# Key copies of attention and indexer: the second partition half written by a DMA instead of by casts and subtractions

## The chip, the cores and the metric

One core of a Trainium2 chip runs the whole kernel. The metric is device time in microseconds from start to end of one execution; where a single number is given for a kernel it is the median of the runs shown. The engines are named PE (TensorE), DVE (VectorE), ACT (ScalarE), POOL (GpSimd) and SP (SyncE).

## The reference

One transformer layer, everything in float32, with 512 tokens and 2048 channels:

```python
h = rms_norm(x, norm_attn[l]) * (1.0 + sc1) + sh1
qa, ka, va, qb, ckv, qi, ki, wi = jnp.split(h @ w_in[l], SPLIT_POINTS, axis=-1)
...
out_a = swa_attention(qa, ka, va, attn_sinks[l], rel_a)
out_b = dsa_attention(qb, ckv, w_uk[l], w_uv[l], qi, ki, wi, rel_b)
mix = jnp.concatenate([out_a, out_b], axis=-1) @ w_out[l]
x = x + g1 * mix
h = rms_norm(x, norm_ffn[l]) * (1.0 + sc2) + sh2
x = x + g2 * conv_ffn(h, w_up[l], conv_w[l], conv_b[l], w_down[l])
```

The six vectors sh1, sc1, g1, sh2, sc2, g2 are silu(c) times a 2048 × 12288 matrix, the modulation weights. Group A has 16 query heads of 64 channels on 2 key heads, with a sliding window of 128. Group B has 16 heads of 64 channels whose keys come from a latent of 256 channels through a matrix of each head, and each query attends to 256 keys at most. Which ones they are is decided by the indexer: 16 small query heads against one key head of 64 channels, a weighted sum of relu(dots), and a top-k of the sums.

## The kernel before, in words

Each float32 operand of a product is split into a high half, rounded to the type that PE multiplies at full rate, and a low half, the rest. A product is three matmuls: high × high, high × low, low × high.

For the scores there is a shorter form. A head has 64 channels, and PE contracts over 128 partitions. `stack_q` therefore puts the high half of a head's queries in one set of 64 partitions and the low half in the other. The keys stand in all 128 partitions, twice the same 64 rows, once for the high half (`kh`) and once for the low half (`kl`). `score` needs two matmuls then: stacked queries × `kh` and stacked queries × `kl`. So each key head is wanted in both partition halves. `dup_k` makes it: two casts on ACT (lines 626 and 627) write the high half into the two partition halves, and two subtractions on DVE (lines 629 and 630) write the low half. It is called 19 times: once for the indexer's keys `ki`, out of PSUM; twice for the A-heads' keys `ka`, out of SBUF; and twice, once a head, for each pair of B-heads `kb0` to `kb7`, out of PSUM.

The stages by time in the trace: to 190 us the first projections; to 290 us the indexer's dot products (`dots`) and first A-heads; to 384 us the top-k on DVE (lines 685 and 688, tiles `top` and `wk`) beside the other A-heads (scores `sca`, weights `sa`, transposed weights `tpa` and `eta`) and the first B-head projection; to 570 us eight pairs of B-heads; then the output projection, the up projection to 1700 us and the down projection to the end.

A pair i of B-heads runs like this. The projection makes its queries (`qb`). `prep_gen` makes the keys in PSUM (`kbp`) and calls `dup_k` for each head. The scores (`scb`) follow, then the softmax on DVE and ACT (`sb`); the weights are transposed by PE into PSUM (`tpb`), copied by ACT to SBUF (`etb`, line 826), and multiplied with the values (`o`). While one pair is in its softmax, PE computes the projection of the next. The two heads of a pair come one after the other.

The order of the work on each engine is made by a scheduler at build time, from priorities and from estimated durations; at run time each engine runs its list in order, and waits. A stream of modulation weights runs beside all of this: POOL issues transfers of 512 KB (`mraw`, line 1520) into a ring of three buffers, and DVE sums them up (`macc`, line 231). POOL issues the next one when DVE has freed a buffer.

The tile of the B-heads' keys has one buffer. Keys of the next pair are written when the scores of the last one are done.

Of the kernel before, what the change touches and what calls it, by code (L numbers as in the profile page):

```python
# [8 lines left out]
F32 = mybir.dt.float32  # L9
F32R = mybir.dt.float32r  # L10
AF = mybir.ActivationFunctionType
OP = mybir.AluOpType
# [21 lines left out]
def hybrid_trunk(ctx, tc, xT, cT, wm, bm, nrm, wik, wiq, wi1, sinks, kvn, wuk, wuv, rel, onehot,  # L34
                 wo, wup, cw, cb, wdn, out):
    nc = tc.nc
    act, dve, pe, pool, sp = nc.scalar, nc.vector, nc.tensor, nc.gpsimd, nc.sync
# [46 lines left out]
    def bank(tag, name, shape=(P, T)):  # L84
        if tag == "sc":
            sc_turn[0] += 1
            tag = f"sc{sc_turn[0] % 3}"
        return psp.tile(list(shape), F32, tag=tag, bufs=banks.get(tag, 1), name=name)
# [63 lines left out]
    def toeplitz(g, head, n):  # L152

        return bass.AP(tensor=biasd.tensor, offset=biasd.offset + 2048 * (HEADS * g + head) + 384 * g + P - 1,
                       ap=[[1024 - 64, 2], [-1, 64], [1, n]])

    ki_ps = bank("acc", "ki_ps")
# [10 lines left out]
    def split(raw, lo, n, name):  # L168
        hi_t = ring.tile([P, 512], F32R, tag="whi", bufs=4, name=f"{name}h")
        lo_t = ring.tile([P, 512], F32R, tag="wlo", bufs=4, name=f"{name}l")  # L170
        act.copy(hi_t[:, :n], raw[:, lo:lo + n])
        dve.tensor_tensor(lo_t[:, :n], raw[:, lo:lo + n], hi_t[:, :n].bitcast(F32), OP.subtract)
        return hi_t, lo_t

    def mm3(ps, wh, wl, ah, al, start, stop):
        pe.matmul(ps, wh, ah, start=start, stop=False)
        pe.matmul(ps, wh, al, start=False, stop=False)
        pe.matmul(ps, wl, ah, start=False, stop=stop)
# [7 lines left out]
    def rstd_of(*a, **k):  # L186
        return list(rstd_parts(*a, **k))[1]
# [26 lines left out]
    def split_to(hi_t, lo_t, full, keep=False):  # L214
        hi = act.copy(hi_t, full)  # L215
        if keep:
            tc.keep_in_program_order(hi)
        dve.tensor_tensor(lo_t, full, hi_t.bitcast(F32), OP.subtract)  # L218
# [77 lines left out]
    def start(gen, delay=0, low=False):  # L296
        def run():
            for _ in range(delay):
                yield
            yield from gen  # L300
        (idle if low else active).append(run())
# [301 lines left out]
    def tp_ps(name, shape=(P, 4, P)):  # L603
        return bank("tp", name, shape)

    def tmp_t(name, shape=(P, T)):
        return p1.tile(list(shape), F32, tag="tmp", bufs=2, name=name)

    def stack_q(ps, scale, name):
        q = p1.tile([P, 2, T], F32R, tag="q", bufs=2, name=name)  # L610
        for h in range(2):
            own, other = slice(64 * h, 64 * h + 64), slice(64 - 64 * h, 128 - 64 * h)
            act.mul(q[own, h], ps[own], scale)
            dve.scalar_tensor_tensor(q[other, h], ps[own], scale, q[own, h].bitcast(F32),
                                     OP.mult, OP.subtract)
        return q
# [5 lines left out]
            pe.matmul(ps, identr, hide, start=False, stop=False)  # L622
        pe.matmul(ps, q[:, h, qc], kl[:, k0:k1], start=False, stop=True)

    def dup_k(src, row, kh, kl):
        act.copy(kh[0:64], src)
        act.copy(kh[64:128], src)
        o = kh[row:row + 64]
        dve.tensor_tensor(kl[0:64], src, o.bitcast(F32), OP.subtract)
        dve.tensor_tensor(kl[64:128], src, o.bitcast(F32), OP.subtract)  # L630

    ETS = 4

# [1 line left out]
    ki = p1.tile([P, 4, T], F32R, tag="k", bufs=1, name="ki")  # L635
# [83 lines left out]
    va = p1.tile([P, NB, P], F32, name="va")  # L719
    ka = p1.tile([P, 4, T], F32R, tag="ka", bufs=1, name="ka")  # L720
    wit = tmp_t("wit", (16, T))
    dup_k(ki_ps[0:64], 0, ki[:, 0], ki[:, 1])
    act.mul(wit, ki_ps[64:80], 1.0 / 32.0)

    def keys_gen():
        cf, csq = [], []
        for i in range(2):
            cf.append(p1.tile([P, T], F32, tag="s", bufs=2, name=f"cf{i}", padded_shape=[P, 1280]))
            csq.append(p1.tile([P, T], F32, tag="et", bufs=ETS, name=f"csq{i}"))
            act.activation(csq[i], key_ps[f"ckv{i}"], AF.Square)  # L730
            act.copy(cf[i], key_ps[f"ckv{i}"])
        kar = p1.tile([P, T], F32, tag="et", bufs=ETS, name="kar")
        act.copy(kar, key_ps["ka"])
        vat = p1.tile([P, T], F32, tag="et", bufs=ETS, name="vat")
        act.copy(vat, key_ps["va"])
        yield
        krs = p1.tile([P, T], F32, tag="et", bufs=ETS, name="krs")
        act.copy(krs, rstd_of(csq, 256, "kvss", lambda n: tp_ps(n, (P, T)), krs))
        for g in range(2):
            dup_k(kar[64 * g:64 * g + 64], 64 * g, ka[:, 2 * g], ka[:, 2 * g + 1])  # L740
        yield
        tps = tp_ps("vatp")
        for b in range(NB):
            pe.transpose(tps[:, b], vat[:, P * b:P * b + P], ident)
        dve.tensor_copy(va, tps)
        for i in range(2):
            dve.scalar_tensor_tensor(cf[i], cf[i], kvn_sb[:, i:i + 1], krs, OP.mult, OP.mult)
            split_to(ch[:, i], cl[:, i], cf[i])
        yield
# [122 lines left out]
    def out_box(i):  # L872
        box = {}

        def get():
            if "t" not in box:
                box["t"] = bank("o", f"o{i}")
            return box["t"]

        def finish():  # L880
            if i < 8:
                mixa[i] = ix.tile([P, T], F32, tag=f"m{i}", name=f"mixa{i}")
                act.copy(mixa[i], get())
                return
            if "mh" in env:
                split_to(env["mh"][:, i], env["ml"][:, i], get())
                env["kept"].add(i)
                return
            mx = tmp_t(f"mx{i}")
            act.copy(mx, get())  # L890
            act.dma_start(mixd[i], mx)
        return get, finish
# [13 lines left out]
    kb, vb = {}, {}  # L906

    def prep_gen(i):
        wr = p1.tile([P, 2 * P], F32, tag="wuk", bufs=1, name=f"wukr{i}")
        sp.dma_start(wr, wuk[i].rearrange("p a b -> p (a b)"))  # L910
        if i % 2 == 0:
            wv = tmp_t(f"wuvr{i}")
            sp.dma_start(wv, wuv[i // 2].rearrange("p a b -> p (a b)"))
        yield
        wh, wl = split(wr, 0, 2 * P, f"wuk{i}")
        yield
        kp = tp_ps(f"kbp{i}", (P, T))
        for r in range(2):
            c = slice(P * r, P * r + P)
            mm3(kp, wh[:, c], wl[:, c], ch[:, r], cl[:, r], r == 0, r == 1)  # L920
        k = p1.tile([P, 4, T], F32R, tag="k", bufs=1, name=f"kb{i}")
        for h in range(2):
            own = slice(64 * h, 64 * h + 64)
            dup_k(kp[own], 64 * h, k[:, h], k[:, 2 + h])
        kb[i] = k
        yield
        if i % 2:
            return
        wh, wl = [t.rearrange("p (a b) -> p a b", a=2) for t in split(wv, 0, 512, f"wuv{i}")]
        yield  # L930
        v = p1.tile([P, NB, 2 * P], F32, tag="v", bufs=2, name=f"vb{i}")
        for half in range(2):
            vp = tp_ps(f"vbp{i}_{half}", (P, 2, 2 * P))
            for b in range(2):
                kc = slice(P * (2 * half + b), P * (2 * half + b) + P)
                for r in range(2):
                    pe.matmul(vp[:, b], ch[:, r, kc], wh[:, r], start=r == 0, stop=False)
                    pe.matmul(vp[:, b], ch[:, r, kc], wl[:, r], start=False, stop=False)
                    pe.matmul(vp[:, b], cl[:, r, kc], wh[:, r], start=False, stop=r == 1)
            act.copy(v[:, 2 * half:2 * half + 2], vp)  # L940
            yield
        vb[i], vb[i + 1] = v[:, :, :P], v[:, :, P:]

    def b_after(i):
        def f(ps):
            q = stack_q(ps, -0.125, f"qb{i}")
            get, finish = out_box(8 + i)
            spans = [(0, 0, 128), (128, 0, 256), (384, 0, 384), (768, 0, 512)]
            heads = [Head(f"b{2 * i + h}", toeplitz(1, 2 * i + h, 512), q, h, kb[i][:, h], kb[i][:, 2 + h], spans,
                          3e38, None, keep, lambda kt, h=h: vb[i][:, kt, 64 * h:64 * h + 64]) for h in range(2)]  # L950
            start(pair_gen(heads, get, finish))
            if i < 7:
                start(prep_gen(i + 1), 1)
        return f
# [572 lines left out]

    start(ahead(index_gen(), 0))
    start(ahead(keys_gen(), 0))
    drive(slots, 0, marks["qb0"] - 4, True)  # L1530
    start(prep_gen(0))
    drive(slots, marks["qb0"] - 4, marks["qb0"], True)
    while idle:
# [212 lines left out]
```

## Time and profile before

| what | value |
|---|---|
| median of 3 runs | 2137.85 us (2136.5 to 2139.96) |
| the profiled execution | 2141.57 us, span 2139.8 us |
| granted clock of TensorE, mean | 0.992 |
| PE busy | 2085.0 us, 97% |
| DVE busy | 1714.8 us, 80% |
| ACT busy | 1139.9 us, 53% |
| POOL busy | 180.8 us, 8% |

A row of the timeline has the start in us, the duration in us, engine, line, operation and tiles, and in brackets the idle time of the engine ahead of it with what ended it. A row of groups has busy time and the mean of one, or, in the view of one tile, the shortest, median and longest duration in ns and the first and last start. A row of stages has the busy time of each engine in a stretch, the granted clock, the share of DMA engines that were busy, and GB/s. Matmuls overlap in the pipeline, so that the duration of one is longer than its distance to the next.

### The profile page before, as it was taken

How to read it: one execution, taken by the hardware profiler on the slowest of the kernel's cores; microseconds unless marked ns; L12 is line 12 of the kernel's file. 1: busy time of each engine (PE TensorE's matmuls, PEld its weight loads, DVE VectorE, ACT ScalarE, POOL GpSimd, SP SyncE). 2: the span in 40 equal slices, each digit the busy share in tenths (PEclk: the TensorE clock that was granted, in tenths of full speed). 3: DMA queues.
4: the chain of work that ended last, by engine and by line, in shares of the span. 5: the costliest groups of instructions: out<-in, count | busy, mean ns of one | idle time of the engine just before them, and what ended most of it. 6: DMA issues, size and time to landing. Idle time of an engine off the chain costs nothing.

```text
span 2139.8 us, 34491 instructions
## 1 busy us (share of the span) xinstructions
PE 2085.0 (97%) x13336; PEld 1834.3 (86%) x13336; DVE 1714.8 (80%) x2522; ACT 1139.9 (53%) x1907; POOL 180.8 (8%) x310
## 2 busy tenths in 40 slices
PE   7999999999999999999999999999999999999987
PEld 4777877777788879999999999999999787777877
DVE  3887899878878788888788888888887897787857
ACT  5324886777722274444444444444444576566544
POOL 0000000111133200000000000000000011111110
PEclk9999999999999999999999999999999999999999
DMA  9773222666699724444444434435434788899883
GB/s 391 272 288 106 55 72 60 193 212 208 197 372 321 235 78 142 155 138 129 148 123 149 148 116 151 149 114 157 139 114 147 272 246 212 225 218 225 207 216 99
DMA packets 125029, 385.18 MB, mean 180 GB/s; under 512 B 14783, under 2 KB 24015, under 8 KB 118080
## 3 DMA queue, kind: packets, MB, share of 16 engines
q1 hardware_dynamic: 84096, 257.16, 36.5%
q0 software_dynamic: 31264, 108.51, 19.4%
q10 hardware_dynamic: 9504, 17.31, 2.1%
q8 instruction: 104, 1.70, 0.3%
q14 instruction: 61, 0.50, 0.1%
HBM read 324.46 MB, written 58.46 MB: 179 GB/s over the span
## 4 chain that ended last, share of the span: by engine, by line
PE 75%; DVE 8%; DMA 7%; issue 5%; ACT 4%; POOL 0%; SPq 0%; DVEq 0%; POOLq 0%; ACTq 0%
PE ux L53 22%; PE uy L53 11%; PE p L53 11%; PE uz L53 6%; PE qip L53 4%; DMA qd<-in_wdn_dram 3%; DMA mraw<-in_wm_dram 2%; DVE wd L218 2%; DMA rawbd<-in_wdn_dram 1%; PE ckv L53 1%; PE mrow L53 1%; DVE wk L688 1%; PE o L53 1%; PE mps L53 1%; DVE top L685 1%
## 5 line engine op out<-in xcount | busy, mean ns | idle before, releaser
L53 PE MATMUL p<-wd,af 128*128 128x512 f32 x1680 | 387.8, 392 | 11.6 <-DVE wd L218 10.6
L53 PEld LDWEIGHTS p<-wd,af 128*128 128x128 f32 x1680 | 314.9, 188 | 84.2 <-DVE wd L218 16.8
L53 PE MATMUL ux<-t_up,wu 128*128 128x256 f32 x2952 | 375.2, 283 | 0.0
L53 PEld LDWEIGHTS ux<-t_up,wu 128*128 128x128 f32 x2952 | 362.9, 192 | 0.9 <-DVE gt L1157 0.2
L53 PE MATMUL uy<-h2h,wu 128*128 128x256 f32 x1312 | 249.6, 283 | 0.0
L53 PEld LDWEIGHTS uy<-h2h,wu 128*128 128x128 f32 x1312 | 210.6, 192 | 0.0
L231 DVE SCALAR_TENSOR_TENSOR macc<-mraw,c_sb,macc 128x512 f32<-128x512 f32 x240 | 179.7, 749 | 10.7 <-DMA mraw<-in_wm_dram 8.7
L53 PE MATMUL uy<-h2l,wu 128*128 128x256 f32 x656 | 185.7, 283 | 0.0
L218 DVE TENSOR_TENSOR wu<-ra,wu 128x1024 fp32r<-128x1024 f32 x82 | 100.4, 1224 | 63.0 <-ACT wu L215 63.0
L215 ACT CAST wu<-rb 128x1024 fp32r<-128x1024 f32 x82 | 86.1, 1051 | 111.3 <-PE ux L53 63.4
L215 ACT CAST wu<-ra 128x1024 fp32r<-128x1024 f32 x82 | 85.7, 1045 | 100.7 <-PE uy L53 62.6
L53 PEld LDWEIGHTS uy<-h2l,wu 128*128 128x128 f32 x656 | 126.0, 192 | 0.0
L53 PE MATMUL uz<-h2h,wu 128*128 128x256 f32 x656 | 124.8, 283 | 0.0
L53 PE MATMUL ux<-h2h,wu 128*128 128x256 f32 x656 | 124.8, 283 | 0.0
L218 DVE TENSOR_TENSOR wu<-rb,wu 128x1024 fp32r<-128x1024 f32 x82 | 100.2, 1222 | 8.5 <-ACT wu L215 8.5
L53 PEld LDWEIGHTS ux<-h2h,wu 128*128 128x128 f32 x656 | 105.3, 192 | 0.0
L53 PEld LDWEIGHTS uz<-h2h,wu 128*128 128x128 f32 x656 | 105.3, 192 | 0.0
L218 DVE TENSOR_TENSOR wu<-rd,wu 128x1024 fp32r<-128x1024 f32 x41 | 50.3, 1226 | 65.4 <-ACT wu L215 65.4
L1525 POOL DMA_DIRECT2D mraw<-in_wm_dram x64 | 34.3, 537 | 800.5 <-DVE macc L231 621.7
L1337 ACT COPY ev<-p 128x512 f32<-128x512 f32 x140 | 81.6, 584 | 22.9 <-PE p L53 21.0
L215 ACT CAST wu<-rs 128x1024 fp32r<-128x1024 f32 x41 | 43.1, 1051 | 95.1 <-DVE rs L1089 53.2
L53 PE MATMUL ux<-h2l,wu 128*128 128x256 f32 x328 | 92.8, 283 | 0.0
(1739 smaller groups left out, 4801.0 us busy)
## 6 DMA issues: line engine op xcount, KB each, us to landing
mraw<-in_wm_dram POOLq DMA_DIRECT2D x160, 256.0 KB, 5.4
total<-ev POOLq DMA_DIRECT2D x70, 512.0 KB, 8.8
mraw<-in_wm_dram SPq DMA_DIRECT2D x32, 1024.0 KB
mraw<-in_wm_dram POOLq DMA_DIRECT2D x48, 512.0 KB, 6.5
ra<-in_wup_dram SPq DMA_DIRECT2D x41, 512.0 KB
rc<-in_wup_dram SPq DMA_DIRECT2D x41, 512.0 KB
rb<-in_wup_dram SPq DMA_DIRECT2D x41, 512.0 KB
rd<-in_wup_dram SPq DMA_DIRECT2D x41, 512.0 KB
```

The lines of the kernel that those rows point to most:

```text
L53: return self.to.matmul(out, w, x, **kw)
L215: hi = act.copy(hi_t, full)
L218: dve.tensor_tensor(lo_t, full, hi_t.bitcast(F32), OP.subtract)
L231: tc.keep_in_program_order(dve.scalar_tensor_tensor(acc, t, cact[:, kt:kt + 1], acc, OP.mult, OP.add))
L685: dve.max(top[b][:, r], cur[b])
L688: dve.match_replace(wk[b], top[b][:, r], cur[b], -3e38)
L1337: act.copy(e[:, b], ps)
L1525: pool.dma_start(t, wm[g, kt // 4][:, kt % 4])
```

## The change

`dup_k` now makes one cast and one subtraction, into the 64 partitions that the source stands in, and POOL issues one DMA that copies high and low half together into the other 64 partitions. For this the two halves of a key lie side by side in the tile, 2 × 512 elements per partition.

```diff
-    def dup_k(src, row, kh, kl):
-        act.copy(kh[0:64], src)
-        act.copy(kh[64:128], src)
-        o = kh[row:row + 64]
-        dve.tensor_tensor(kl[0:64], src, o.bitcast(F32), OP.subtract)
-        dve.tensor_tensor(kl[64:128], src, o.bitcast(F32), OP.subtract)
+    def dup_k(src, row, k):
+        own, other = slice(row, row + 64), slice(64 - row, 128 - row)
+        act.copy(k[own, 0], src)
+        dve.tensor_tensor(k[own, 1], src, k[own, 0].bitcast(F32), OP.subtract)
+        pool.dma_start(k[other], k[own])
...
-    dup_k(ki_ps[0:64], 0, ki[:, 0], ki[:, 1])
+    dup_k(ki_ps[0:64], 0, ki[:, 0:2])
...
-            dup_k(kar[64 * g:64 * g + 64], 64 * g, ka[:, 2 * g], ka[:, 2 * g + 1])
+            dup_k(kar[64 * g:64 * g + 64], 64 * g, ka[:, 2 * g:2 * g + 2])
...
-            dup_k(kp[own], 64 * h, k[:, h], k[:, 2 + h])
+            dup_k(kp[own], 64 * h, k[:, 2 * h:2 * h + 2])
...
-            heads = [Head(f"b{2 * i + h}", toeplitz(1, 2 * i + h, 512), q, h, kb[i][:, h], kb[i][:, 2 + h], spans,
+            heads = [Head(f"b{2 * i + h}", toeplitz(1, 2 * i + h, 512), q, h, kb[i][:, 2 * h], kb[i][:, 2 * h + 1], spans,
```

Below line 630 the line numbers of the changed kernel are one less. The scheduler orders the work anew, and three places moved.

The first is PE in the stage of the B-heads, where the weights of pair 1 are transposed (`tpb2_0` and `tpb3_0` are the transposes of its two heads) between the matmuls of a later projection (`qb3ps`). Before:

```order
L57 MATMUL tpb2_0_4278<-identr_77,sb2_4086 128x128 x4
L53 MATMUL qb3ps_4264<-h1h1_65,qb3r_1h_4127 128x512
L53 MATMUL qb3ps_4264<-h1l1_69,qb3r_1h_4127 128x512
L53 MATMUL qb3ps_4264<-h1h1_65,qb3r_1l_4128 128x512
L53 MATMUL qb3ps_4264<-h1h1_65,qb3r_1h_4127 128x512
L53 MATMUL qb3ps_4264<-h1l1_69,qb3r_1h_4127 128x512
L53 MATMUL qb3ps_4264<-h1h1_65,qb3r_1l_4128 128x512
L53 MATMUL qb3ps_4264<-h1h1_65,qb3r_1h_4127 128x512
L53 MATMUL qb3ps_4264<-h1l1_69,qb3r_1h_4127 128x512
L53 MATMUL qb3ps_4264<-h1h1_65,qb3r_1l_4128 128x512
L57 MATMUL tpb3_0_4285<-identr_77,sb3_4178 128x128 x4
```

And now:

```order
L57 MATMUL tpb2_0_4269<-identr_77,sb2_4079 128x128 x4
L53 MATMUL qb3ps_4255<-h1h1_65,qb3r_1h_4120 128x512
L53 MATMUL qb3ps_4255<-h1l1_69,qb3r_1h_4120 128x512
L53 MATMUL qb3ps_4255<-h1h1_65,qb3r_1l_4121 128x512
L57 MATMUL tpb3_0_4276<-identr_77,sb3_4171 128x128 x4
```

The second head's transposes stand after three matmuls of the projection instead of nine; the six others follow them. The same happens to the transposes of the pairs before and after: nine and three matmuls for pair 0, ten and five for pair 2, eleven and five for pair 3, ten and five for pair 4.

The second is ACT at the same time, when the keys of pair 2 are made and the weights of pair 1 are copied out of PSUM. `qb2` are the stacked queries, `qb3r` and `wuvr2` weights that are being split. Before:

```order
L626 CAST kb2_4241<-kbp2_4234 64x512
L627 CAST kb2_4241<-kbp2_4234 64x512
L613 ACTIVATE qb2_4253<-qb2ps_4006 64x512
L171 CAST qb3r_3h_4260<-qb3r_3_4125 128x512
L171 CAST wuv2h_4292<-wuvr2_4113 128x512
L626 CAST kb2_4241<-kbp2_4234 64x512
L627 CAST kb2_4241<-kbp2_4234 64x512
L613 ACTIVATE qb2_4253<-qb2ps_4006 64x512
L826 COPY etb2_0_4279<-tpb2_0_4278 128x512
```

And now:

```order
L627 CAST kb2_4234<-kbp2_4227 64x512
L613 ACTIVATE qb2_4244<-qb2ps_3999 64x512
L171 CAST qb3r_3h_4251<-qb3r_3_4118 128x512
L627 CAST kb2_4234<-kbp2_4227 64x512
L613 ACTIVATE qb2_4244<-qb2ps_3999 64x512
L171 CAST wuv2h_4283<-wuvr2_4106 128x512
L825 COPY etb2_0_4270<-tpb2_0_4269 128x512
```

Two casts are gone ahead of the copy of the transposed weights, one for each head.

The third is POOL, which issues the stream of modulation weights (`mraw9_12` and so on) and now the copies. Before:

```order
L1520 DMA mraw9_8_4156<-in_wm_dram 128x1024
L1520 DMA mraw9_10_4207<-in_wm_dram 128x1024
L1520 DMA mraw9_12_4250<-in_wm_dram 128x1024
L1520 DMA mraw9_14_4300<-in_wm_dram 128x1024
```

And now:

```order
L1519 DMA mraw9_8_4149<-in_wm_dram 128x1024
L1519 DMA mraw9_10_4200<-in_wm_dram 128x1024
L1519 DMA mraw9_12_4241<-in_wm_dram 128x1024
L629 DMA kb2_4234<-kb2_4234 64x1024 x2
L1519 DMA mraw9_14_4291<-in_wm_dram 128x1024
```

The two copies of a pair stand between two transfers of modulation weights. On PE, the first score of a pair's first head now waits for the first copy, and that of the second head for the second.

## The prediction

> **What bounds the kernel now.** I read the page first, then the busy time of each engine by stage, then the PE timeline around the stages that use the copied keys. The page's engine line and chain line say that TensorE is the bound almost everywhere:
>
> ```profile
> PE 2085.0 (97%) x13336; PEld 1834.3 (86%) x13336; DVE 1714.8 (80%) x2522; ACT 1139.9 (53%) x1907; POOL 180.8 (8%) x310
> PE 75%; DVE 8%; DMA 7%; issue 5%; ACT 4%; POOL 0%; SPq 0%; DVEq 0%; POOLq 0%; ACTq 0%
> ```
>
> PE is idle for 2139.8 − 2085.0 = 54.8 us in all, and the edit touches nothing that PE computes. So whatever it brings or takes must show in PE gaps near the three users of the keys. The keys of the indexer and of the A-heads are made near 190 to 206 us, the B-heads' from 352 to 560 us. The stage view (columns: us, PE, PEld, DVE, ACT, POOL busy, granted clock, DMA share, GB/s) gives the two stretches with the B-heads' keys:
>
> ```profile
> 350.00:384.00 34.00, 27.62 (x154) 21.45 (x152) 32.75 (x103) 24.62 (x71) 0.00 (x0) 0.90 0.15 43
> 395.00:570.00 175.00, 172.30 (x1096) 139.92 (x1095) 143.10 (x316) 135.82 (x323) 22.17 (x42) 1.00 0.68 213
> ```
>
> In the first, DVE is busy 32.75 of 34.00 us and PE waits for it: this is the end of the top-k chain, and keys of pair 0 are cast in its middle. In the second PE is busy 172.30 of 175.00, so all its gaps together are 2.70 us. These are the gaps, in order of time:
>
> ```profile
> 366.97 0.48 PE L57 MATMUL tpa<-identr,sa 128*128 128x128 f32 x1 [2.29 <-ACT sa L818]
> 379.22 1.13 PE L57 MATMUL tpa<-identr,sa 128*128 128x128 f32 x4 [1.75 <-ACT sa L818]
> 382.62 0.79 PE L53 MATMUL qb0ps<-h1h,qb0r_3l 128*128 128x512 f32 x1 [2.27 <-DVE qb0r_3l L172]
> 412.38 0.66 PE L57 MATMUL tpb<-identr,sb 128*128 128x128 f32 x4 [0.60 <-ACT etb L826]
> 435.58 0.66 PE L57 MATMUL tpb<-identr,sb 128*128 128x128 f32 x4 [0.42 <-ACT etb L826]
> 461.90 0.66 PE L57 MATMUL tpb<-identr,sb 128*128 128x128 f32 x4 [0.51 <-ACT etb L826]
> 485.49 0.66 PE L57 MATMUL tpb<-identr,sb 128*128 128x128 f32 x4 [0.63 <-ACT etb L826]
> 511.15 0.66 PE L57 MATMUL tpb<-identr,sb 128*128 128x128 f32 x4 [0.49 <-ACT etb L826]
> ```
>
> The first three belong to the DVE-bound stage, 6.31 us. The last five are one place, repeated once per pair of B-heads: the second head's first transpose waits until ScalarE has copied the first head's transposed weights out of PSUM. They sum to 2.65 us, nearly all of the 2.70.
>
> **The change part by part.** It removes one cast and one subtraction at each of 19 places. The rows of the B-heads' keys give the durations:
>
> ```profile
> L627 ACT CAST kb<-kbp x16: 578/580/584, 353.2 to 558.4; 64x512 fp32r<-64x512 f32 x16
> L629 DVE TENSOR_TENSOR kb<-kbp,kb x16: 673/688/695, 359.0 to 559.1; 64x512 fp32r<-64x512 f32 x16
> L630 DVE TENSOR_TENSOR kb<-kbp,kb x16: 683/689/695, 359.7 to 559.9; 64x512 fp32r<-64x512 f32 x16
> ```
>
> So 19 × 0.58 = 11.0 us of ScalarE and 19 × 0.69 = 13.1 us of VectorE go. Only the part of it that ends a PE gap counts.
>
> *Pair 0, in the top-k chain.* Two subtractions, 2 × 0.69 = 1.38 us, leave DVE before the split that PE waits for:
>
> ```profile
> 381.88 0.69 DVE L172 TENSOR_TENSOR qb0r_3l<-qb0r,qb0r_3h 128x512 fp32r<-128x512 f32 x1
> ```
>
> Its end and the gap of 2.27 us that it closes are both later than the two subtractions (359.0 to 363.4), and DVE has only 1.25 us of idle time in the 34 us. The other two gaps there wait for a softmax that DVE's reciprocals release, so they move with it. Bounds: 0, if another wait takes over, to −1.38. I take −1.3, because DVE is the engine with nothing to spare.
>
> *Pairs 1 to 5, the transposes.* I name each place by the pair whose keys are made there; the weights transposed are those of the pair before. In pair 2 the work is this:
>
> ```profile
> 430.43 0.56 ACT L626 CAST kb<-kbp 64x512 fp32r<-64x512 f32 x1
> 431.01 0.58 ACT L627 CAST kb<-kbp 64x512 fp32r<-64x512 f32 x1
> 434.94 0.58 ACT L826 COPY etb<-tpb 128x512 f32<-128x512 f32 x1
> 432.47 0.60 PE L57 MATMUL tpb<-identr,sb 128*128 128x128 f32 x4
> 433.37 0.40 PE L53 MATMUL qb3ps<-h1h,qb3r_1l 128*128 128x512 f32 x1
> 434.76 0.40 PE L53 MATMUL qb3ps<-h1h,qb3r_1l 128*128 128x512 f32 x1
> ```
>
> ScalarE works without a pause from 430.43 to the copy at 434.94; two casts fewer bring that copy 2 × 0.58 = 1.16 us earlier, to 433.78, ending at 434.36. With the old order of PE the gap of 0.42 would close. But the order of PE is not the old one: the waiting transpose now stands after three matmuls and not after nine. PE gets there after the matmul of 433.37, which ends at 433.77, instead of the one of 434.76, which ends at 435.16. It asks 1.39 us earlier (six matmuls, 0.23 each) and is served 1.16 us earlier, so the gap becomes 0.42 + 1.39 − 1.16 = 0.65 us. By the same count, pairs 1 and 4 have their transpose moved six matmuls up (+0.23 each), and pairs 3 and 5 five (5 × 0.23 = 1.15, no change). Sum 3 × 0.23 = +0.7 us. Bounds: −2.65, if ScalarE's copies come early enough to close all five in spite of the order, to +3.6, if only one of the two casts counts (3 × 1.39 + 2 × 1.15 − 5 × 0.58). I take +0.7, which is what the rows of pair 2 give.
>
> *The indexer's and A-heads' keys.* The subtractions end near 194 and 206 us and the first users come much later:
>
> ```profile
> L630 DVE TENSOR_TENSOR ki<-ki_ps,ki x1: 684/684/684, 193.8 to 193.8; 64x512 fp32r<-64x512 f32 x1
> L53 PE MATMUL dots<-ki,qs x96: 277/339/501, 208.7 to 286.5; 128*128 128x256 f32 x32, 128*128 128x384 f32 x32, 128*128 128x512 f32 x32
> L630 DVE TENSOR_TENSOR ka<-kar,ka x2: 685/688/690, 202.7 to 205.4; 64x512 fp32r<-64x512 f32 x2
> L53 PE MATMUL sca<-ka,qa x128: 222/281/387, 228.3 to 376.7; 128*128 128x256 f32 x96, 128*128 128x128 f32 x32
> ```
>
> A copy has some 15 us before the first dot product and 22 us before the first A score, against landings below 9 us (rows further down). PE computes projections meanwhile. I take nothing, gain or loss. If that cover were gone, one whole landing of about 5 us would show.
>
> *The 19 copies.* Each is 64 partitions × 4 KB = 256 KB on POOL's queue, and PE now waits for it. No copy within SBUF stands in the trace. The nearest rows are the stream of modulation weights on the same queue (columns: KB each, median us from issue to landing), and one other transfer of that queue as an upper neighbour, and the issues on POOL:
>
> ```profile
> mraw<-in_wm_dram POOLq DMA_DIRECT2D x160, 256.0 KB, 5.4
> total<-ev POOLq DMA_DIRECT2D x70, 512.0 KB, 8.8
> mraw<-in_wm_dram POOLq DMA_DIRECT2D x48, 512.0 KB, 6.5
> L1520 POOL DMA_DIRECT2D mraw<-in_wm_dram x45: 527/527/556, 385.0 to 566.9; - x45
> ```
>
> An issue takes POOL 0.53 us, and POOL is busy 22.17 of 175 us there, so 19 × 0.53 = 10 us on POOL is hidden. What POOL queues behind a waiting copy is the next modulation weight: in pair 2 the issues before and after stand at 430.68 and 438.44, and the copies would go out near 432 and 434.5, in between. The landing decides, so I count the room in pair 2 and in the tightest one by time, pair 7:
>
> ```profile
> 430.68 0.53 POOL L1520 DMA_DIRECT2D mraw<-in_wm_dram  x1 [6.92 <-DVE macc L231]
> 437.39 0.75 DVE L231 SCALAR_TENSOR_TENSOR macc<-mraw,c_sb,macc 128x512 f32<-128x512 f32 x1
> 438.44 0.53 POOL L1520 DMA_DIRECT2D mraw<-in_wm_dram  x1 [7.23 <-DVE macc L231]
> 438.78 0.47 PE L53 MATMUL scb<-kb,qb 128*128 128x512 f32 x1
> 448.97 0.39 PE L53 MATMUL scb<-kb,qb 128*128 128x512 f32 x1
> 554.51 0.56 ACT L626 CAST kb<-kbp 64x512 fp32r<-64x512 f32 x1
> 562.18 0.48 PE L53 MATMUL scb<-kb,qb 128*128 128x512 f32 x1
> ```
>
> POOL answers 0.30 us after DVE (end of the sum 437.39 + 0.75 = 438.14, issue 438.44). Pair 2: cast ends 430.99, subtraction +0.69, issue near 432.0, first use 438.78, room 6.8 us. Pair 7: 555.07 + 0.69 + 0.30 = 556.1 to 562.18, room 6.1 us. The second head's copy has 10 us more (448.97). The landing of 256 KB, 5.4 us, fits into both. In pair 2 the copy also stands behind 512 KB that went out at 430.68 and whose consumer starts at 437.39; 256 KB more take 6.5 − 5.4 = 1.1 us by the two landing rows, so the copy lands near 438.5, 0.3 us before its use. Bounds: 0, and the 8.8 us of the upper neighbour, with which seven pairs lose about 8.8 − 6.5 = 2.3 us each, 16 us. I take 0, since size and queue are those of the first row.
>
> The Trainium skill, "SBUF — State Buffer", section "Door 1: The DMA port swizzle", speaks against this value: a transfer that spans only 64 partitions reaches half of the SBUF ports, and so half of the rate. No run shown so far has such a transfer. By it the 1.1 us above would be 2.2, the copy of pair 2 would land at 439.6, and a pair as tight as this would lose 0.8 us; with two such pairs the sum would be 1.6 us higher.
>
> *Sum.* −1.3 + 0.7 + 0 + 0 = −0.6 us. The profiled execution took 2141.57 us, with a span of 2139.8, so it would go to 2141.0. It stands 3.7 us above the median of 2137.85, which goes to **2137.2 us**. After 570 us the kernel is the same, and PE is busy throughout most of it, so I let a shift pass unchanged.
>
> **The rivals.** *A* is the forecast.
>
> *B, the copies come late.* Head 0's first score of each pair 1 to 7 waits for the copy; behind it in PE's order stand all the scores and the next projections. It decides from a landing of about 6.5 us on, the mean of the rooms, and is measurable from (4.3 + 0.6) / 7 = 0.7 us beyond that, 7.2 us. For it: the queue carries 512 KB right ahead of the copy, with landings of 6.5 us. Against it: the landing of 5.4 us for this size. At 8.8 us: 2137.2 + 16 = 2153 us.
>
> *C, ScalarE's relief reaches PE in full.* The five gaps close although the order asks earlier: −1.3 − 2.65 = −4.0, 2133.9 us. For it: in the stage ScalarE is busy 135.82 of 175 us, so it may have caught up by more than the two casts where it waits for DVE's subtractions. Against it: in pair 2 it does not pause between cast and copy.
>
> *D, the half clock after the gaps is avoided.* The granted clock falls behind the long gaps:
>
> ```profile
> 367.00:370.00 3.00, 3.00 (x14) 3.00 (x15) 2.91 (x8) 2.30 (x5) 0.00 (x0) 0.50 0.00 0
> 384.00:386.00 2.00, 2.00 (x6) 1.51 (x6) 2.00 (x5) 1.02 (x3) 0.56 (x1) 0.50 0.48 158
> 386.00:388.00 2.00, 2.00 (x11) 1.76 (x10) 2.00 (x4) 0.65 (x2) 0.47 (x1) 0.65 0.72 213
> ```
>
> In 384 to 388, where PE is the bound again, 2 × 0.50 + 2 × 0.35 = 1.7 us are lost. If the gap ahead is shorter by 1.3 us and the clock stays up, the sum is −0.6 − 1.7 = −2.3, 2135.5 us. Against it: gaps of 0.9 us and more would remain. The Trainium skill, "TensorE: Matmul & The Clock Gate", section "Part 1: The HAM clock gate", has the clock halved by an idle window of a free-running monitor; by that a gap's place in time can matter as much as its length, and D can come out either way.
>
> **How the numbers follow.** A has 0.60, B 0.20, C 0.13, D 0.07. A measurement of this kernel can tell about 0.2%, 4.3 us, from no change: faster is below 2133.6, slower above 2142.1. A puts 0.05 below and 0.03 above, since its terms' smaller bounds reach that far only together; B puts 0.17 above; C 0.09 below, for 2133.9 is on the line and D's clock may join it; D 0.03 below. That is faster 0.17, same 0.63, slower 0.20. The range for 8 in 10 goes from 2133.0, a little past C, to 2143.5, past copies that are late by 0.9 us in seven pairs.
>
> **What would show it.** Pair 0: the split of the fourth quarter of that projection (381.88 now) 1.3 us earlier. Transposes: the five gaps still there, 0.5 to 0.85 us, for a copy by ScalarE that starts 1.1 us earlier. Copies: landings of 5 to 6.5 us, and no PE gap at the first score of a pair; a gap there named after a DMA would be B. The forecast is wrong if those gaps exceed 0.7 us, if the five transposes run without a gap, or if stages behind 570 us take back or add more than a microsecond.

## The result and the profile after

The changed kernel takes 2155.98 us (2151.86 to 2161.51, 4 runs) against 2137.18 us before (2136.28 to 2139.96, 4 runs): the ratio is 1.0082, 95% interval 1.0061 to 1.0102, so it is slower by 0.6 to 1.0%. The forecast was 2137.2 with a range to 2143.5. Rival B, copies that come late, had 2153.

The execution profiled took 2151.86 us with a span of 2150.1, 10.3 us more than the span of before. The page's engine line shows the same work on PE, and one cast and one subtraction fewer at 19 places:

```profile
PE 2083.5 (97%) x13336; PEld 1835.3 (85%) x13336; DVE 1703.1 (79%) x2503; ACT 1130.2 (53%) x1888; POOL 190.8 (9%) x329
```

The stage view of the changed kernel (columns as before: us, PE, PEld, DVE, ACT, POOL busy, granted clock, DMA share, GB/s) puts the loss into the stage of the B-heads. PE was busy 172.30 of its 175 us and is now busy 162.12, and DMA share is up from 0.68 to 0.74:

```profile
395.00:570.00 175.00, 162.12 (x1011) 131.72 (x1012) 127.30 (x284) 121.70 (x292) 28.12 (x53) 0.98 0.74 216
```

Its PE gaps from 365 us to the output projection, in order of time (the row of 392.54 is the first score of pair 0 and has no gap):

```profile
365.11 0.33 PE L57 MATMUL tpa<-identr,sa 128*128 128x128 f32 x1 [0.75 <-ACT sa L817]
376.38 1.29 PE L57 MATMUL tpa<-identr,sa 128*128 128x128 f32 x4 [2.04 <-ACT sa L817]
379.79 0.79 PE L53 MATMUL qb0ps<-h1h,qb0r_3l 128*128 128x512 f32 x1 [2.11 <-DVE qb0r_3l L172]
392.54 0.40 PE L53 MATMUL scb<-kb,qb 128*128 128x512 f32 x1
402.57 0.50 PE L53 MATMUL kbp<-ch,wuk1h 128*128 128x512 f32 x1 [0.72 <-ACT wuk1h L171]
408.60 0.63 PE L57 MATMUL tpb<-identr,sb 128*128 128x128 f32 x4 [0.49 <-DVE kb L628]
415.00 0.50 PE L53 MATMUL scb<-kb,qb 128*128 128x512 f32 x1 [1.64 <-DMA kb<-kb]
441.31 0.50 PE L53 MATMUL scb<-kb,qb 128*128 128x512 f32 x1 [3.44 <-DMA kb<-kb]
468.81 0.49 PE L53 MATMUL scb<-kb,qb 128*128 128x512 f32 x1 [0.66 <-DMA kb<-kb]
494.01 0.50 PE L53 MATMUL scb<-kb,qb 128*128 128x512 f32 x1 [2.67 <-DMA kb<-kb]
518.97 0.50 PE L53 MATMUL scb<-kb,qb 128*128 128x512 f32 x1 [0.24 <-DMA kb<-kb]
526.66 0.93 PE L53 MATMUL o<-etb,vb 128*64 128x128 f32 x8 [0.38 <-ACT etb L825]
540.12 0.63 PE L57 MATMUL tpb<-identr,sb 128*128 128x128 f32 x4 [2.32 <-DVE kb L628]
572.22 0.50 PE L53 MATMUL scb<-kb,qb 128*128 128x512 f32 x1 [0.71 <-DMA kb<-kb]
585.74 0.80 PE L53 MATMUL wo0ps<-ml,wo0r_2h 128*128 128x512 f32 x1 [6.68 <-DVE ml L218]
```

Six first scores wait for their copy, 9.36 us in all. The view of the key tile has the landings, and the same sum among its waits (times in ns for the issue, then us and number of waits):

```profile
L629 POOL DMA_DIRECT2D kb<-kb x16: 513/520/527, 359.7 to 567.4; - x16
...
  PE scb L53: 9.4, 6
...
DMA to landing us min/median/max: 6.0/7.2/10.2
```

The last gap, 6.68 us, is another load. DVE waits 5.31 us for a bias tile that SP issued 21 us earlier, and the split that PE needs stands behind it on DVE:

```profile
562.74 0.51 SPq L775 DMA_DIRECT2D tbb<-biasd  x1
...
583.71 0.69 DVE L802 CUSTOM_DVE_ANT_0 sb<-scb,tbb 128x512 f32<-128x512 f32 x1 [5.31 <-DMA tbb<-biasd]
```

There is a gain as well. The first score of pair 0 starts at 392.54; in the kernel before it was here:

```profile
395.74 0.40 PE L53 MATMUL scb<-kb,qb 128*128 128x512 f32 x1
```

How large the loss is can be read in the output projection. Here are the whole stretch from 395 to 605 us and one group of matmuls behind the B-heads, in each pair the kernel before first:

```profile
395.00:605.00 210.00, 206.65 (x1279) 166.85 (x1279) 165.64 (x358) 153.46 (x361) 30.71 (x58) 1.00 0.68 219
395.00:605.00 210.00, 189.73 (x1179) 153.88 (x1179) 143.85 (x321) 139.06 (x334) 29.19 (x55) 0.96 0.70 204
L53 PE MATMUL wo4ps<-mh,wo4r_0h x4: 389/389/389, 615.9 to 617.9; 128*128 128x512 f32 x4
L53 PE MATMUL wo4ps<-mh,wo4r_0h x4: 389/389/389, 633.8 to 635.9; 128*128 128x512 f32 x4
```

The first score comes 3.2 us earlier, and the output projection 17.9 us later. Between them PE is idle for 20.3 us instead of 3.3: the 9.4 at first scores, the 6.7 at 585.74 (before there were 0.64 us at that place, 570.96), 2.8 at two transposes, and small gaps. That accounts for 17 of the 21 us. The rest fits the granted clock, 0.96 in the mean instead of 1.00, which takes 0.04 × 210 = 8 us at most; a part of it falls into the gaps.

The 17.9 us come near the 18.8 between the medians. The profiled execution, the fastest of the four, ends only 10.3 us later than that of before. It is 14.6 us behind at the first matmul of the down projection (1662.5 and 1677.1 us), and the other 4 us are made up there. Two executions of one kernel, profiled in the experiments below, took 466.8 and 470.6 us from there to the end, so the ends of two single executions can differ by several us for reasons of that stage alone.

### The profile page after: what moved, and what is told of

The parts are those of the page before. It is cut to its first block, busy times and chain, and to the rows that moved or that the text cites. A ratio compares the mean times of both kernels' runs of the same rounds, so it can differ in the third digit from the quotient of the medians.

```text
span 2150.1 us, 34504 instructions
## 1 busy us (share of the span) xinstructions
PE 2083.5 (97%) x13336; PEld 1835.3 (85%) x13336; DVE 1703.1 (79%) x2503; ACT 1130.2 (53%) x1888; POOL 190.8 (9%) x329
## 4 chain that ended last, share of the span: by engine, by line
PE 77%; DMA 9%; DVE 8%; ACT 3%; issue 3%; POOL 0%; SPq 0%; DVEq 0%; ACTq 0%; POOLq 0%
PE ux L53 22%; PE p L53 11%; PE uy L53 11%; PE uz L53 5%; PE qip L53 4%; DMA tbb<-biasd 2%; DMA qd<-in_wdn_dram 2%; DMA rawbd<-in_wdn_dram 2%; DMA kb<-kb 2%; DVE wd L218 1%; PE ckv L53 1%; PE mrow L53 1%; DVE wk L687 1%; DVE top L684 1%; PE mps L53 1%
```

## The experiments

Each time is compared with runs of the kernel before from the same chip. Theory W says that the loss is the wait of first scores for late copies. Rival T says that it is the added traffic, rival S that it is the moved order of PE.

**One half of the change at a time.** The DMA copy for the indexer, the A-heads and pair 0 alone, and for pairs 1 to 7 alone:

```diff
+        if copy:
+            pool.dma_start(k[other], k[own])
+        else:
+            act.copy(k[other, 0], src)
+            dve.tensor_tensor(k[other, 1], src, k[own, 0].bitcast(F32), OP.subtract)
...
-            dup_k(kp[own], 64 * h, k[:, 2 * h:2 * h + 2])
+            dup_k(kp[own], 64 * h, k[:, 2 * h:2 * h + 2], i == 0)
```

> The DMA copy is kept for the indexer's keys, the A-heads' keys and pair 0 of the B-heads; pairs 1 to 7 go back to two casts and two subtractions. Theory W (the loss is the wait of each pair's first score for a copy that lands 7 to 10 us after its issue): no such wait is left, and the 3.2 us by which the first B score came earlier (395.74 to 392.53) stay: ratio 0.9985, about 2134 us. Rival T (the loss is the added traffic, which makes other loads late, the bias tiles above all): 5 copies of 19 remain, none near 570 us: also about 2134 to 2137 us. Rival S (the loss comes with the moved order of PE): order as before in pairs 1 to 7, no change.

> The complement: the DMA copy for pairs 1 to 7 of the B-heads alone. Theory W and rival T: the gain of 3.2 us is lost and the whole loss stays, 19 + 3 = 22 us over before, about 2159 us; PE gaps at the first score of a pair named after the copy.

The first part alone took 2132.51 us against 2134.29, ratio 0.9990 (0.9975 to 1.0005); the second 2156.10, ratio 1.0108 (1.0079 to 1.0137). The whole loss, 21.8 us where 22 were expected, belongs to pairs 1 to 7. In the profile of the second part first scores wait as in the change:

```profile
  PE scb L53: 9.1, 6
```

Since the interval of the first part held both no change and my 0.9985, it was timed again.

> The DMA copy for the indexer, the A-heads and pair 0 alone, once more with more rounds: the 2.2 us by which its first B score came earlier (395.74 to 393.53) against a scatter of about 0.1%: ratio 0.9985 to 1.0000, about 2 us faster than before.

It was 2131.19 against 2135.36 us, ratio 0.9976 (0.9962 to 0.9989): faster, by more than expected.

**Another engine, another queue.** The copy by POOL's own engine, and the DMA from SP's queue:

```diff
-        pool.dma_start(k[other], k[own])
+        pool.tensor_copy(k[other], k[own])
```

```diff
-        pool.dma_start(k[other], k[own])
+        sp.dma_start(k[other].bitcast(F32), k[own].bitcast(F32))
```

> The copy into the other partitions is made by POOL's own engine, one instruction for each head, in place of the DMA; everything else as in the change. Theory W: the wait shrinks from 7 to 10 us to the time of one POOL instruction of 1024 elements a partition, which no row shows yet; from the 0.29 us for 128 elements in the row of its masking operation, up to 2.3 us. The room is 6.1 to 6.8 us, so no wait: 2134 us or a little less. Rival T: no added traffic either: the same. Rival S (the moved order of PE): the loss of the change stays, over 2145 us.

> The same DMA copies, issued by SP on its queue instead of POOL's, so that they don't stand behind 512 KB of modulation weights. Theory W with the queue as its cause: landings near the 3.0 to 4.8 us of the A-heads' copies, at most one or two PE gaps at first scores, about 2135 us. Theory W with the DMA engines' load as its cause: landings and gaps as in the change, 2150 us and more. Rival T: the traffic is the same as in the change, 2150 us and more, with the loss at the bias tiles.

With POOL's engine 2135.29 us, ratio 1.0004 (0.9991 to 1.0017). The copy takes 1.04 us and no first score waits. PE has the same order of work as in the change, and the loss is gone; rival S falls with that. The expected gain is missing; seven waits of transposes for the second subtraction, 4.5 us, take its place:

```profile
L629 POOL CAST kb<-kb x16: 1036/1041/1365, 359.9 to 559.3; 64x1024 fp32r<-64x1024 f32 x16
...
  PE tpb L57: 4.5, 7
```

From SP's queue 2182.34 us, ratio 1.0232 (1.0213 to 1.0251). First scores wait four times as long as in the change, so a copy is late also where it doesn't stand behind modulation weights on POOL's queue:

```profile
  PE scb L53: 38.6, 7
```

**Traffic without waits, and less traffic.** The kernel before with 19 transfers that nobody reads:

```diff
+    scr = dram.tile([P, 2, T], F32R, name="scr")
...
+        pool.dma_start(scr[other], k[own])
```

> Two casts and two subtractions as before, and beside them the same 19 transfers of 256 KB from the same places on POOL's queue, into a buffer in DRAM that nothing reads or waits for. Theory W (the waits of the first scores for the copies make the loss): no wait, so within 0.2% of before, 2135 to 2139 us. Rival T (the added traffic makes other loads late): a loss of 6 us or more, with PE or DVE waiting for bias tiles or weights: 2143 us and more.

It took 2133.73 us, ratio 0.9991 (0.9979 to 1.0004). The traffic alone costs nothing that can be measured, and DVE waits for no bias tile; rival T falls in that form. The landings of these transfers are shorter than those of the copies, 5.6 against 7.2 us in the middle:

```profile
DMA to landing us min/median/max: 2.9/5.6/7.3
```

The change with half of the modulation weights on POOL's queue:

```diff
-            pool.dma_start(two[0], wm[g, kt // 4][:, kt % 4:kt % 4 + 2])
-        return two[0][:, kt % 2]
+            pool.dma_start(two[0][:, 0], wm[g, kt // 4][:, kt % 4])
+        return two[0][:, 0]
```

> The change, with the stream of modulation weights on POOL's queue cut from 512 KB to 256 KB an issue in the stage of the B-heads (the second half of each is left out, the first is used twice). Theory W with the load of the DMA engines and the queue ahead as the cause of late landings: landings of the B copies fall from 6.3 to 10.2 us to 4.5 to 7, and the PE gaps at first scores from 9.1 us in all to under 3. Rival L (a copy between two places in SBUF takes this long by itself): landings stay at 6 to 10 us, gaps as in the change.

One run, 2135.57 us, in a stage that moves fewer bytes, so that it is not to be read as a gain. What counts is the landing, and its median stayed where it was. The waits fell from 9.4 to 5.8 us, where the cause that I had in mind should have left under 3:

```profile
  PE scb L53: 5.8, 4
...
DMA to landing us min/median/max: 5.0/7.2/9.6
```

**Half a copy, two copies.** The DMA copies the low half alone; and each DMA twice:

```diff
-        pool.dma_start(k[other], k[own])
+        act.copy(k[other, 0], src)
+        pool.dma_start(k[other, 1], k[own, 1])
```

```diff
         pool.dma_start(k[other], k[own])
+        pool.dma_start(k[other], k[own])
```

> The DMA copies the low half alone, 128 KB; the high half is cast twice by ScalarE as before. Theory W: packets of a copy take half the time, landings fall by 0.7 us or more, and the gaps at first scores by 3 to 6 of their 9 us: about 2148 to 2152 us. Rival L: landings and gaps as in the change, 2156 us.

> The change, with each copying DMA issued twice in a row, and the scores waiting for both. Theory W: the second copy lands 1.4 us or more behind the first (64 packets of about 0.34 us over 16 engines), and in each of seven pairs the first score waits that much longer: 10 us or more over the change, about 2166 us. Rival S (the loss is the moved order of PE, not the landing): under 4 us more.

With half a copy 2137.45 us, ratio 1.0004 (0.9993 to 1.0014), one wait of 0.8 us at a first score. I had expected 3 to 6 us less of the waits, and 2148 us or more. A landing that is 0.8 us shorter in the median took away nearly all of them; the room is about 6.5 us, and landings lie around it:

```profile
  PE scb L53: 0.8, 1
...
DMA to landing us min/median/max: 3.0/6.4/8.4
```

With two copies one run of 2198.91 us. My number was too small by a mistake in the design: the second copy writes the same bytes, so POOL issued it only when the first had landed (its wait is the first row), and a pair waited for two landings in a row. What it shows agrees with theory W: what is added to the landing shows at the first scores.

```profile
  POOL kb L630: 48.2, 14
  PE scb L53: 48.0, 7
```

**Why the landings are long.** In the profile of the change I had passed over stretches like these two, 18 us after the bias tile of 425.97 us was issued:

```profile
444.00:446.00 2.00, 2.00 (x11) 1.81 (x11) 0.70 (x2) 0.59 (x2) 0.00 (x0) 0.73 0.12 47
446.00:448.00 2.00, 2.00 (x15) 1.47 (x16) 1.82 (x8) 2.00 (x7) 0.00 (x0) 1.00 0.13 49
```

A share of 0.12 to 0.13 is two of 16 DMA engines at work (2 / 16 = 0.125), at 47 to 49 GB/s. The same share stands just ahead of 583.7 us, where the bias tile of 562.74 lands:

```profile
580.00:582.00 2.00, 0.00 (x0) 0.00 (x0) 0.00 (x0) 0.84 (x2) 0.00 (x0) 0.91 0.13 48
582.00:584.00 2.00, 0.00 (x0) 0.00 (x0) 0.29 (x1) 0.00 (x0) 0.00 (x0) 0.50 0.12 43
```

The bias tile of a B-head is read from DRAM as two groups of 64 slanted rows. If a group goes to one engine, 256 KB sit on two engines, and any transfer that is spread over 16 lands only when its share on these two is through. That was theory W2, and the first test replaced the source by 128 plain rows of another tensor, which leaves the bias out of the result:

```diff
-            sp.dma_start(self.tb[:, :self.nt], self.tb_src)
+            sp.dma_start(self.tb[:, :self.nt], wm[0, 0][:, 0] if self.nt == T else self.tb_src)
```

> The change, with each B-head's bias tile (256 KB) loaded from 128 plain rows of another tensor in place of the two slanted groups of 64 rows; the bias is left out by that, and the bytes are the same. In the change, stretches with only two of 16 DMA engines at work (share 0.12 to 0.13, 45 to 49 GB/s) follow these loads. Theory W2 (two engines hold the bias tile's packets, and a copy lands when its part on these two is through): landings of the B copies fall from 6.3 to 10.2 us to 4 to 6.5, PE gaps at first scores to under 2 us in all, no DVE wait for a bias tile: 2132 to 2139 us. Rival L (a copy within SBUF is slow by itself) or rival Q (the 512 KB ahead on the queue): landings and gaps as in the change, 2150 us and more.

> The kernel before with the same plain bias loads, as the measure for the run above. No PE gap of before waits for a bias tile, so within 0.2% of before; a gain of several us here would mean that a part of the gain above has nothing to do with the copies.

The change with plain rows: 2130.40 us, ratio 0.9973 (0.9958 to 0.9988). The kernel before with them: 2132.44, ratio 0.9988 (0.9974 to 1.0002). The median landing of the copies fell by half, with the same copies, the same queue, the same bytes and the same order of work on PE, and no first score waited:

```profile
DMA to landing us min/median/max: 2.9/3.6/6.6
```

The second test keeps the bias and changes only the number of groups. The table is written to DRAM eight times instead of twice, and a tile is read as 8 groups of 16 rows:

```diff
-    biasd = dram.tile([32, 2, 1024], F32, name="biasd")
+    COPIES = 8
+    biasd = dram.tile([32, COPIES, 1024], F32, name="biasd")
...
-                       ap=[[1024 - 64, 2], [-1, 64], [1, n]])
+                       ap=[[1024 - P // COPIES, COPIES], [-1, P // COPIES], [1, n]])
```

> The change, with the bias table written eight times instead of twice to DRAM, so that a bias tile is loaded as 8 groups of 16 rows instead of 2 groups of 64; all results as in the change. Theory W2 (a group of rows goes to one DMA engine, and two engines held up the copies): landings of the B copies fall from 6.3 to 10.2 us to 3 to 7, PE gaps at first scores to under 1.5 us in all, no wait for a bias tile: 2128 to 2137 us, ratio 0.997 to 1.000. If it was not the two groups but the slant or the tensor: landings and gaps as in the change, ratio over 1.006.

> The kernel before with the bias loaded as 8 groups. No PE gap of before waits for a bias tile; the plain rows gave 0.9988. Theory W2: 0.9975 to 1.0005.

> The DMA copy for the indexer, the A-heads and pair 0 alone, with the bias loaded as 8 groups. If the copies of pairs 1 to 7 bring something once the bias loads don't hold them up, this is slower than e10 by 1 to 3 us; if they bring nothing, the two are equal within 0.1%: ratio 0.997 to 0.999.

| kernel, with 8 groups | median us | ratio to before | interval |
|---|---|---|---|
| the change | 2129.06 | 0.9972 | 0.9962 to 0.9982 |
| the kernel before | 2129.84 | 0.9984 | 0.9973 to 0.9996 |
| the copy for indexer, A-heads and pair 0 alone | 2124.41 | 0.9958 | 0.9944 to 0.9972 |

All three are faster than before (2134.01 us on that chip). In the change the landings are those of the run with plain rows, and from 395 to 570 us three PE gaps over 0.25 us are left. The third, 1.19 us at 563.70, stands at the place of the 6.68 of the change, and DVE waits for no bias tile any more:

```profile
DMA to landing us min/median/max: 2.9/3.6/6.7
```

```profile
407.65 0.63 PE L57 MATMUL tpb<-identr,sb 128*128 128x128 f32 x4 [0.51 <-DVE kb L629]
525.51 0.63 PE L57 MATMUL tpb<-identr,sb 128*128 128x128 f32 x4 [0.31 <-DVE kb L629]
563.70 0.50 PE L53 MATMUL wo0ps<-ml,wo0r_2h 128*128 128x512 f32 x1 [1.19 <-DVE ml L219]
```

So the cause of the late landings is the two groups. The version with the copy for pair 0 alone is the fastest that was run and beats both kernels. I had expected it equal to the full change or slower by 1 to 3 us; it is 4.7 us faster, though the intervals overlap. The stage of the B-heads doesn't explain that. These are the first matmuls of the down projection in the two profiles, the full change first:

```profile
L53 PE MATMUL p<-wd,af x1680: 387/389/501, 1653.5 to 2052.1; 128*128 128x512 f32 x187
L53 PE MATMUL p<-wd,af x1680: 387/389/504, 1658.2 to 2046.6; 128*128 128x512 f32 x187
```

The full change is 4.7 us ahead there, and behind at the end of the span (2129.4 against 2123.1 us). So in these two executions the copies of pairs 1 to 7 do bring something once the bias loads don't hold them up, and the down projection, whose work neither edit touches, takes it back. Whether that is scatter or would last over more executions is open.

## Why the prediction was wrong, point by point

**What bounds the kernel** was right: PE. But not all of the loss lies in gaps at the users of the keys, where the prediction looked for it: 6.0 us are a late bias tile, and a part is the granted clock that falls behind such gaps.

**The copies, taken at 0,** is the step that failed. The room was right: 406.58 to 415.00 less the wait of 1.64 is 6.8 us for pair 1, and by the same count 6.3 to 6.8 us for the others against 6.1 to 6.8 forecast. So was POOL's part, 0.52 us an issue. The landing was not: I took 5.4 us, from other transfers of that size on the same queue, and the copies of the change took 6.0 to 10.2, with a median of 7.2 that is longer than the room. That row is a median over transfers of later stages, which load no bias tiles; the first copy of each pair from 1 on goes out 2.5 to 6.5 us behind one. The neighbour that mattered was not a row of POOL's queue but SP's bias loads, and the prediction never asked on how many DMA engines each load runs. I also named the wrong neighbour, the 512 KB ahead of a copy on POOL's queue: with 256 KB there the median landing stayed at 7.2 us.

The Trainium skill, "DMA: Bandwidth & Descriptors", section "Why a DMA increments its semaphore by 16 and not by 1", says that the number of engines follows from the slowest dimension of the access pattern; a pattern of two groups gets two. The traces agree: 0.12 to 0.13 of 16 engines with two groups, and with eight the copies' median landing is 3.6 us instead of 7.2. What the prediction took from the Trainium skill, "SBUF — State Buffer", section "Door 1: The DMA port swizzle", half the ports for 64 partitions, is neither borne out nor refuted: pair 0's two copies in the version that has them alone among the B-heads, with 8 groups, land in 2.8 to 3.2 us, and no run copied the same bytes over 128 partitions.

**Rival B** was the right mechanism with 0.20 of the chance, and its time of 2153 us was close, but by another sum: not seven waits of 2.3 us, but six of 0.2 to 3.4 us, together 9.4, and the late bias tile, 6.0, which the prediction did not have, with the lower clock on top. With eight groups neither is waited for, which is why I count both to the same two engines.

**Pair 0, taken at −1.3,** was right for the gaps, but the first score came earlier by more: 3.2 us in the change, 2.2 and 3.3 in the two profiles of the part alone (393.53 and 392.42). The three gaps ahead of it sum to 4.90 us now, 1.41 less than the 6.31 of before. The time went out of the first one, ahead of the transposes, 2.29 to 0.75 us, and hardly out of the one that the prediction named, 2.27 to 2.11. Most of the rest is the clock, a form of rival D, which had 0.07. Behind the first gap it was 0.50 from 367 to 370 us, and now it is 1.00:

```profile
367.00:370.00 3.00, 3.00 (x27) 2.14 (x26) 2.94 (x10) 1.94 (x4) 0.00 (x0) 1.00 0.03 5
```

That is worth 0.50 × 3 = 1.5 us. Rival D expected it behind the last gap, and there nothing was saved: the half clock only came earlier with the work, and from 376 to 395 us the mean is 0.82 before and after:

```profile
376.00:395.00 19.00, 14.90 (x81) 11.24 (x81) 16.25 (x40) 12.36 (x36) 1.61 (x3) 0.82 0.56 182
376.00:395.00 19.00, 16.44 (x88) 12.69 (x89) 15.38 (x32) 10.22 (x25) 2.15 (x4) 0.82 0.62 198
```

**The transposes, taken at +0.7,** had the wrong cause in the new order. I let the second head's transposes wait for the copy of the first head's out of PSUM, as before. With the copies unhindered (the change with 8 groups, pair 2) they start while that copy is still running, and wait 0.17 us for the second subtraction, which frees another PSUM bank:

```profile
429.35 0.69 DVE L629 TENSOR_TENSOR kb<-kbp,kb 64x512 fp32r<-64x512 f32 x1
...
429.93 0.59 ACT L826 COPY etb<-tpb 128x512 f32<-128x512 f32 x1
...
430.19 0.63 PE L57 MATMUL tpb<-identr,sb 128*128 128x128 f32 x4 [0.17 <-DVE kb L629]
```

There two gaps above 0.25 us, 0.82 together, and smaller ones like this stand in place of five of 2.65. So rival C's gain is real in part, up to 1.8 us, by a release that I had not looked at. Part of that belongs to the 8 groups: the kernel before with them has three such gaps, 1.53 us, and against it the gain is 0.7. In the change itself two gaps of 2.81 us stand in the same place, so nothing of it was left.

**The indexer's and A-heads' copies, taken at nothing,** hold: no PE gap above 0.25 us near 209 or 228 us.

**The stages behind 570 us, taken to pass a shift unchanged,** did not. In the two profiled executions 17.9 us in the output projection became 14.6 at the down projection and 10.3 at the end. The prediction had set one microsecond as a sign of being wrong. What takes it back was not traced.

## What to carry to other kernels

When a wait moves onto a transfer, its landing time can depend on all transfers that share DMA engines with it, here on another queue; ask of each of them over how many engines it is spread, and look for stretches in which the DMA share stands at a small multiple of one sixteenth. A load that nobody waits for can be the reason why a new one is late: here taking it off the two engines gained the kernel before 0.2%, and turned the change from 0.8% slower into 0.3% faster. And a transfer that has 15 us of room was free here, while seven with 6.5 us of room were not, even though the medians of other transfers' landings looked short enough.

## What was not expected of the hardware

Two DMA engines drained 47 to 49 GB/s alone for 4 us while the others idled, and a bias tile of 256 KB in two groups took 21 us to land. The granted clock fell to half (0.50) behind a PE gap of 2.29 us in the kernel before, and stayed at 1.00 behind one of 2.67 us in the change (494.01), so the length of a gap alone does not decide it. Copying 64 partitions of 1024 elements into the other 64 took POOL's engine 1.04 us, and a DMA about 3 us where nothing held it up (2.8 to 3.2 for pair 0 in the version of it alone with 8 groups) and up to 10.2 in the change. The same DMA from SP's queue, which also carries the bias tiles, made the first scores wait 38.6 us in place of 9.4.
